# Hybrid decoder layer on one core: weight low parts and row products all on VectorE, output-projection weights in four quarters

## The chip, the cores and the metric

The kernel runs on 1 core of one Trainium2 chip. The metric is the device time of one execution in microseconds (us); lower is better. The engines of the core run in parallel, each working through its own queue in order: TensorE (PE, matmuls; PEld its weight loads), VectorE (DVE), ScalarE (ACT), GpSimd (POOL), and SyncE (SP), which issues the DMA transfers. They wait for one another through semaphores.

## The reference, cut to what matters

One decoder layer over 512 tokens of width 1024: a mixer with two attentions, a cross-attention into 256 memory rows, a mixture of experts, a final norm.

```python
h = _rms_norm(x, g_mix[l])
fq, fk, fv, f_logit, dq, dk, dv, gate_a, gate_b = jnp.split(h @ w_in[l], offsets, axis=-1)
...
y_a = _merge_heads(_fox_attention(...))      # 8 heads
y_b = _merge_heads(...)                      # 4 differential heads, rotary
merged = (jax.nn.sigmoid(gate_a) * (y_a @ w_branch_a[l])
          + jax.nn.sigmoid(gate_b) * (y_b @ w_branch_b[l]))
x = x + merged @ w_out[l]
x = x + _cross_attention(_rms_norm(x, g_cross[l]), _rms_norm(mem, g_mem[l]), w_cq[l], w_ckv[l], w_co[l])
hm = _rms_norm(x, g_ffn[l]).reshape(b * s, d)
x = x + _hier_moe(hm, ...).reshape(b, s, d)  # 32 experts, top 2
return _rms_norm(x, g_final)
```

## The kernel before

**Split products.** The big products ahead of the experts are done as three matmuls each (`mm3`, lines 278 to 280): both factors are cut in a high part and a low part. ACT makes the high part (`activation Copy`, L176), and a subtraction makes the low part (L177, `split`). For weights these are called `wh` and `wl`, for activations `hh`/`hl`, `mh`/`ml` and so on.

**The weight stream.** The class `Stream` (object `W`) cuts each weight into chunks of 1 MB and each chunk into two halves of 128x1024 elements. `load` has SP fetch a half into a raw buffer `wr`; `split` makes `wh` on ACT and `wl` either on VectorE or, for the halves whose number is in `self.pool`, on GpSimd. The set holds the numbers 12 to 63 without 57 and 59. `use(i, j)` makes sure that a chunk is split and asks, in `more`, for the next one. For the query weight of the cross-attention (`c_cq`) GpSimd also multiplies the raw half by a gain for each row (L143).

**Order.** It is written out by hand. At the start `nat_unit` runs four token tiles through the first weight chunk while `h_gain` (L326) multiplies the transposed input by `g_mix`, `h_split` makes its parts, and `h_stat` makes the row factors `rT`, which the small product `pR` spreads (L370). Then a loop of 24 iterations runs: 16 of `Fox` (4 head pairs by 4 query blocks of 128), 8 of `Diff`. Each does scores, softmax, multiplies of the probabilities by the reciprocal (L592 for Fox; L698 and L699 for Diff), a projection unit of weights (`unit()`, two in Diff), `W.more()`, the transposes `tf` or `td` (L275) and their copies (`pf` L603, `pd` L711), and the product with v one iteration later. Units of the first output branch (`br`, evacuated at L846) lie in the Diff iterations, so does `finish`, which transposes `zn` (`tz`, L745). After the loop come the remaining gate units and branch units; the last four branch units leave `mh` and `ml`, the merged activations, behind (L846, L853, L856, L857).

**The output projection.** `out_unit` adds `merged @ w_out` to x for token tile t and columns 256c to 256c+255: 8 contraction tiles by 3 matmuls of 256 columns into half a PSUM bank `wop` (tag "a", two buffers), then the addition (L1018). For c = 0 the tiles 0 and 1 go together. Tiles 2 and 3 are fillers: a list of steps as words (`U20` is `out_unit(2, 0)`) mixes them with the cross-attention (T, N, Q, K, S, M, P, A, O) and the routing. `W` in that list splits `c_co`. Then the experts run: 1 MB pages come through a ring of buffers, which PE frees, and PE multiplies them (`gu` L1410, `yd` L1432, `cb` L1450, `ga` L1238).

Of the kernel before, what the change touches and what calls it, by code (L numbers as in the profile page):

```python
# [10 lines left out]
F32 = mybir.dt.float32  # L11
# [4 lines left out]
OP = mybir.AluOpType  # L16
AX = mybir.AxisListType

P = 128
# [3 lines left out]
KD = D // P  # L23
# [15 lines left out]
def tile_hybrid_block(  # L39
# [5 lines left out]
    V, A, PE, G = nc.vector, nc.scalar, nc.tensor, nc.gpsimd  # L45
# [10 lines left out]
    def page(shape, dt, name):  # L56
        return pgp.tile(list(shape), dt, name=name, tag="pg")
# [3 lines left out]
    def work(shape, dt, name, tag="w"):  # L61
        return wk.tile(list(shape), dt, name=name, tag=tag, bufs=bufs[tag])
# [10 lines left out]
    def bank(name, tag):  # L73
        return ps.tile([P, 512], F32, name=name, tag=tag, bufs={"a": 2, "s": 4, "y": 2}[tag])
# [8 lines left out]
    def xt(t):  # L83
        return X[t // 2][:, t % 2]
# [6 lines left out]
    gm = c1.tile([P, KD], F32, name="gm")  # L91
# [14 lines left out]
    def xT(t, k0=0, n=KD):  # L106
        return XT[t // 2][:, t % 2, k0:k0 + n]
# [8 lines left out]
    class Stream:  # L116
        def __init__(self):
            self.spec, self.raw, self.hl = [], {}, {}
            self.loaded = self.done = self.next = 0
            self.lazy = False  # L120
            self.pool = set(range(12, 64)) - {57, 59}
            self.scale, self.new, self.land, self.ahead = {}, {}, {}, {}

        def add(self, src, k, n):
# [3 lines left out]
        def load(self, upto):  # L128

            while self.loaded < min(upto, 2 * len(self.spec), self.done + self.ahead.get(self.loaded // 2, NLD)):  # L130
                i, j = divmod(self.loaded, 2)
                src, k, n = self.spec[i]
                sl = slice(j * k // 2, (j + 1) * k // 2)
                if i in self.land:
                    if j == 0:
                        self.land[i] = page([P, k, n], F32, f"wr{i}")
                    raw = self.land[i][:, sl]
                else:
                    raw = work([P, k // 2, n], F32, f"wr{i}{j}", "ld")
                self.raw[self.loaded] = raw  # L140
                nc.sync.dma_start(raw, src[:, sl])
                if i in self.scale:
                    G.tensor_tensor(raw, raw, self.scale[i][:, sl, None].to_broadcast([P, k // 2, n]), op=OP.mult)  # L143
                self.loaded += 1

        def split(self, upto):

            while self.done < min(upto, 2 * len(self.spec)):
                i, j = divmod(self.done, 2)
                self.load(self.done + 1)  # L150
                _, k, n = self.spec[i]
                if j == 0:
                    self.hl[i] = [self.new.get((i, u), page)([P, k, n], F32R, f"w{u}{i}") for u in "hl"]
                hi, lo = self.hl[i]
                sl = slice(j * k // 2, (j + 1) * k // 2)
                n = k // 2 // 2 if self.done < 2 else k // 2
                for k0 in range(0, k // 2, n):
                    d = slice(sl.start + k0, sl.start + k0 + n)
                    split(hi[:, d], lo[:, d], self.raw[self.done][:, k0:k0 + n], G if self.done in self.pool else V)
                self.done += 1  # L160
                self.load(self.done + 4)

# [9 lines left out]

            self.split(self.next)

    def split(hi, lo, src, E=V):
        A.activation(hi, src, AF.Copy)  # L176
        E.tensor_tensor(lo, src, hi.bitcast(F32), op=OP.subtract)  # L177

    W = Stream()

# [96 lines left out]
    def mm3(o, lh, ll, rh, rl, first, last):  # L277
        PE.matmul(o, lh, rh, start=first, stop=False)  # L278
        PE.matmul(o, lh, rl, start=False, stop=False)  # L279
        PE.matmul(o, ll, rh, start=False, stop=last)  # L280
# [14 lines left out]
    def nat_unit(chunk, t, dst, d0, name, nt=1, tag="a"):  # L295

        wh, wl = W.use(chunk, t // 2)
        o = bank(f"{name}p{t}", tag)
        for i in range(nt):
            sl = slice((t + i) * P, (t + i + 1) * P)  # L300
            gemm(o[:, 256 * i:256 * i + 256], KD, lambda k: hk(HH, k, sl), lambda k: hk(HL, k, sl),
                 lambda k: wh[:, k, :], lambda k: wl[:, k, :])

        def evac():
            for i in range(nt):
                A.activation(dst[:, t + i, d0:d0 + 256], o[:, 256 * i:256 * i + 256], AF.Copy, scale=rT[:, t + i:t + i + 1])

        return evac
# [9 lines left out]
    def h_split(t, qs=(0, 1)):  # L318

        sl = slice(t * P, (t + 1) * P)  # L320
        for q in qs:
            split(HH[q][:, :, sl], HL[q][:, :, sl], xT(t, 4 * q, 4))

    def h_gain(t, E, k0=0, n=KD):
        v = xT(t, k0, n)
        E.tensor_tensor(v, v, gm[:, k0:k0 + n, None].to_broadcast([P, n, P]), op=OP.mult)  # L326

    def h_stat(t):
        rms_stat(xt(t), f"nx{t}", out=rT[:, t:t + 1])
# [5 lines left out]

    W.lazy = True
    lg = c1.tile([P, KD, 16], F32R, name="lg")
    h_gain(0, V, 0, 4)
    h_gain(0, G, 4, 4)
    h_split(0, (0,))  # L340
    W.split(1)
    h_split(0, (1,))
    W.split(2)
    evs = []
    for t in range(NT):
        evs.append(nat_unit(c_fv[0], t, fv, 0, "fv0", tag="as"[t // 2]))
        if t + 1 < NT:
            h_gain(t + 1, G)
            h_split(t + 1)
        if t == 1:  # L350
            split(lg[:, :, 0:8], lg[:, :, 8:16], lg_r)
            W.split(3)
        if t == 2:
            h_stat(0)
            h_stat(1)
            evs.pop(0)()
            evs.pop(0)()
            h_stat(2)
            h_stat(3)
# [474 lines left out]
    MH, ML = {}, {}  # L834
# [68 lines left out]
                for j in range(4):  # L903
                    units.append(lambda br_=br_, c=c, j=j: branch_unit(br_, c // 2, j))
    wov = w_out[0].rearrange("(k p) n -> p k n", p=P)
    c_wo = [W.add(wov[:, :, 256 * c:256 * c + 256], KD, 256) for c in range(4)]
    c_cq = W.add(w_cq[0].rearrange("(k p) n -> p k n", p=P), KD, 256)
    W.scale[c_cq] = gcc
    c_co = W.add(w_co[0].rearrange("(k p) n -> p k n", p=P), 2, D)
# [93 lines left out]

    W.new[c_co, "h"] = page2

    def out_unit(t, c, *more):

        wh, wl = W.hl[c_wo[c]]
        o = {}
        for u in (t, *more):  # L1010
            o[u] = bank(f"wop{c}{u}", "a")[:, 0:256]
            for k in range(KD - 1 if more else KD):
                out_part(o[u], u, wh, wl, k)
        for u in (t, *more):
            if more:
                out_part(o[u], u, wh, wl, KD - 1)
            xs = xt(u)[:, 256 * c:256 * c + 256]
            V.tensor_tensor(xs, o[u], xs, op=OP.add)  # L1018

    def out_part(o, t, wh, wl, k):  # L1020
        sl = slice(t % 2 * P, (t % 2 + 1) * P)
        mm3(o, MH[t // 2][:, k, sl], ML[t // 2][:, k, sl], wh[:, k, :], wl[:, k, :], k == 0, k == KD - 1)


    CX = {}
# [272 lines left out]

    EX = Experts()

    for c in range(4):
        W.use(c_wo[c], 1)
        if c == 0:
            out_unit(0, c, 1)
        else:
            out_unit(0, c)
            out_unit(1, c)
    W.split(2 * c_cq + 2)
    for step in """T0 N0 U20 Q0 U21 K0 T1 N1 U30 U22 W Q1 S0 M0 K1 U23 U31 N2 T2 S1 P0 Q2 M1 U32 A0 U33 K2 T3 O0 N3 S2
        M2 Q3 P1 X0 K3 F0 A1 S3 M3 P2 R0 O1 L0 P3 F1 z0.0 A2 X1 z0.1 A3 O2 z0.2 z0.3 R1 O3 L1 z0.4 z0.5 z1.0  # L1310
        E E E E H0 z0.6 H1 z1.1 z1.2 F3 X2 z0.7 z0.8 z1.3 z1.4 z0.9 z0.10 z1.5 z0.11 z1.6 z1.7 z0.12 z0.13 F2 z1.8
        R2 X3 L2 r0 z1.9 o0 H2 z2.0 z1.10 z1.11 z2.1 z1.12 z2.2 z2.3 z2.4 z1.13 R3 g0.0 z2.5 z2.6 r1 L3 z2.7
        z2.8 g0.1 z3.0 z2.9 o1 z2.10 z3.1 g0.3 z2.11 H3 z3.2 z2.12 z2.13 g0.2 g1.3 z3.3 r2 z3.4 g1.0 g1.1
        z3.5 z3.6 o2 z3.7 z3.8 z3.9 g1.2 z3.10 z3.11 g2.0 z3.12 z3.13 g2.1 g2.3 r3 g2.2 o3""".split():
        f, t = step[0], int(step[1]) if len(step) > 1 else 0
        if f == "U":
            out_unit(t, int(step[2]))
        elif f == "E":
            EX.load(page)
        elif f == "W":  # L1320
            W.split(2 * c_co + 2)
        elif f == "z":
            route_step(t)
        elif f == "g":
            gather0(t, int(step[3]))
        elif f == "M":
            cross_soft(t)
            cross_scale(t)
        else:
            {"N": lambda t: x_stat(t, "nc"), "F": ffn_stat, "r": ranks, "o": lambda t: onehot(0, t), "X": x_trans, "T": cross_trans, "Q": cross_q, "K": cross_qt, "S": cross_scores, "P": cross_ptrans,  # L1330
             "A": cross_av, "O": cross_out, "H": ffn_split, "R": router,
             "L": router_t}[f](t)
# [227 lines left out]
    for p in range(NE // 2):  # L1560
        q, qi = divmod(p, 2)
        more = q + 1 < NE // QUAD
        final = not more and qi == 1
        h = []
        for a in range(2):
            e = 2 * p + a
            sl = slice((2 * qi + a) * CAP, (2 * qi + a + 1) * CAP)
# [211 lines left out]
```

## Time and profile before

| | us |
|---|---|
| median of 3 runs | 1009.11 |
| lowest, highest | 1008.07, 1009.96 |
| the profiled execution, own time | 1009.81 |
| its span | 1008.1 |
| PE busy in the span | 966.5 (96%) |
| DVE busy | 457.2 (45%) |
| ACT busy | 308.6 (31%) |
| POOL busy | 200.3 (20%) |

The profiled execution takes 1.7 us more than its span. Busy shares are means over the span: the part ahead of the experts (to about 520 us) and the part with the experts have different loads. A timeline row gives the start, the length, the engine, the line, the operation, the tiles written and read, and in brackets how long the engine stood idle before it and what released it. A matmul's printed length has its way through the array in it; how fast a stream runs is read from one start to the next.

### The profile page before, as it was taken

How to read it: one execution, taken by the hardware profiler on the slowest of the kernel's cores; microseconds unless marked ns; L12 is line 12 of the kernel's file. 1: busy time of each engine (PE TensorE's matmuls, PEld its weight loads, DVE VectorE, ACT ScalarE, POOL GpSimd, SP SyncE). 2: the span in 40 equal slices, each digit the busy share in tenths (PEclk: the TensorE clock that was granted, in tenths of full speed). 3: DMA queues.
4: the chain of work that ended last, by engine and by line, in shares of the span. 5: the costliest groups of instructions: out<-in, count | busy, mean ns of one | idle time of the engine just before them, and what ended most of it. 6: DMA issues, size and time to landing. Idle time of an engine off the chain costs nothing. (4 is left out here: it accounts for less than half of the span.)

```text
span 1008.1 us, 13868 instructions
## 1 busy us (share of the span) xinstructions
PE 966.5 (96%) x5494; PEld 643.8 (64%) x5495; DVE 457.2 (45%) x967; ACT 308.6 (31%) x672; POOL 200.3 (20%) x245
## 2 busy tenths in 40 slices
PE   8999899999989999999799999999999999999985
PEld 7787677787878898998646536364453635436332
DVE  6554885846562526445632333323233332233335
ACT  5344444444353344245321112021121212112104
POOL 4841122223444555410100000000000000000003
PEclk8999999999999999999899999999999999999998
DMA  8221121121131247237389899999999999999902
GB/s 307 85 65 62 63 63 64 43 85 63 63 126 63 84 131 266 84 126 301 159 324 422 330 423 416 423 421 418 421 421 422 420 419 421 420 421 419 411 12 84
DMA packets 47862, 246.19 MB, mean 244 GB/s; under 512 B 4784, under 2 KB 12208, under 8 KB 23728
## 3 DMA queue, kind: packets, MB, share of 16 engines
q1 hardware_dynamic: 47648, 245.24, 61.4%
q8 instruction: 45, 0.74, 0.3%
q14 instruction: 25, 0.20, 0.1%
q10 hardware_dynamic: 144, 0.00, 0.0%
HBM read 243.13 MB, written 2.10 MB: 243 GB/s over the span
## 5 line engine op out<-in xcount | busy, mean ns | idle before, releaser
L1410 PE MATMUL gu<-gu,xg 128*64 128x512 f32 x960 | 210.5, 593 | 1.7 <-PEq L1479 1.6
L1410 PEld LDWEIGHTS gu<-gu,xg 128*64 128x64 f32 x960 | 72.9, 137 | 133.2 <-issue 121.1
L177 POOL TENSOR_TENSOR wl<-wr,wh 128x1024 fp32r<-128x1024 f32 x50 | 120.6, 2419 | 186.5 <-ACT wh L176 179.4
L1432 PE MATMUL yd<-dn,A 128*64 128x512 f32 x472 | 110.4, 596 | 0.0
L1454 DVE TENSOR_TENSOR xr<-cb,xr 128x512 f32<-128x512 f32 x120 | 75.7, 684 | 50.6 <-PE cb L1450 50.4
L1415 DVE SCALAR_TENSOR_TENSOR A<-A,gu 128x256 f32<-128x256 f32 x32 | 13.5, 421 | 176.1 <-ACT A L1414 176.1
L1550 POOL MEMSET A<- 128x128 f32 x1 | 0.2, 206 | 438.2 <-PE pth L275 438.2
L1432 PEld LDWEIGHTS yd<-dn,A 128*64 128x64 f32 x472 | 34.9, 137 | 64.3 <-issue 63.4
L1414 ACT ACTIVATE A<-gu 128x256 f32<-128x256 f32 x32 | 12.3, 385 | 201.2 <-PE gu L1410 201.2
L176 ACT ACTIVATE wh<-wr 128x1024 fp32r<-128x1024 f32 (+1 forms) x66 | 67.1, 1026 | 8.0 <-POOL wr L143 6.8
L1450 PE MATMUL cb<-Y,ohT 128*128 128x512 f32 x240 | 67.5, 412 | 0.9
L1440 DVE SCALAR_TENSOR_TENSOR Y<-yd,ws,Y 128x512 fp32r<-128x512 f32 x32 | 23.9, 750 | 91.8 <-ACT Y L1439 89.9
L1238 PE MATMUL ga<-G,hnh 128*128 128x256 f32 x256 | 64.6, 290 | 0.2 <-DVE ge L1358 0.2
L1238 PE MATMUL ga<-G,hnl 128*128 128x256 f32 x256 | 62.8, 283 | 0.0
L1439 ACT ACTIVATE Y<-yd,ws 128x512 fp32r<-128x512 f32 x32 | 21.9, 687 | 126.8 <-PE yd L1432 126.8
L1450 PEld LDWEIGHTS cb<-Y,ohT 128*128 128x128 f32 x240 | 42.7, 191 | 12.5 <-DVE xr L1454 3.2
L1238 PEld LDWEIGHTS ga<-G,hnh 128*128 128x128 f32 x256 | 48.5, 190 | 3.1 <-issue 2.4
L1238 PEld LDWEIGHTS ga<-G,hnl 128*128 128x128 f32 x256 | 48.6, 190 | 0.6
L1384 ACT ACTIVATE xg<-ga,smc 128x256 f32<-128x256 f32 x64 | 29.8, 475 | 52.3 <-PE ga L1238 52.3
L278 PE MATMUL wop<-wh,mh 128*128 128x256 f32 x128 | 36.9, 288 | 2.9 <-DVE xr L1018 1.8
L279 PE MATMUL wop<-wl,mh 128*128 128x256 f32 x128 | 36.4, 284 | 0.6 <-POOL wl L177 0.6
L280 PE MATMUL wop<-wh,ml 128*128 128x256 f32 x128 | 36.3, 283 | 0.0
(611 smaller groups left out, 1962.6 us busy)
## 6 DMA issues: line engine op xcount, KB each, us to landing
gu<-in_w_gu_dram SPq DMA_DIRECT2D x120, 1024.0 KB, 12.3
dn<-in_w_dn_dram SPq DMA_DIRECT2D x55, 1024.0 KB, 17.4
wr<-in_w_inp_dram SPq DMA_DIRECT2D x40, 512.0 KB, 3.7
Z<-in_w_gu_dram SPq DMA_DIRECT2D x8, 1024.0 KB, 14.8
wr<-in_w_out_dram SPq DMA_DIRECT2D x8, 512.0 KB, 6.5
Z<-in_w_dn_dram SPq DMA_DIRECT2D x4, 1024.0 KB, 19.8
dn<-in_w_dn_dram SPq DMA_DIRECT2D x6, 512.0 KB, 13.8
x<-in_x_dram SPq DMA_DIRECT2D x2, 1024.0 KB, 11.6
```

The source lines that it names most:

```text
L176: A.activation(hi, src, AF.Copy)
L177: E.tensor_tensor(lo, src, hi.bitcast(F32), op=OP.subtract)
L278: PE.matmul(o, lh, rh, start=first, stop=False)
L279: PE.matmul(o, lh, rl, start=False, stop=False)
L280: PE.matmul(o, ll, rh, start=False, stop=last)
L1238: PE.matmul(o, CX[u, t // 2][:, t % 2, kb * P:(kb + 1) * P], GQ[q][:, t].rearrange("p e s -> p (e s)"), start=(first and u == "h"), stop=( ...
L1384: A.activation(XG[q][:, kb], o, AF.Copy, scale=gfc[:, kb:kb + 1])
L1410: PE.matmul(gu[64 * f:64 * f + 64, :], xg(2 * i + j), w[:, :, j, 256 * f:256 * f + 256], start=(i + j == 0), stop=(i + j == 4))
L1432: PE.matmul(y[j][64 * a:64 * a + 64, :], hT[a][:, f % 2, f // 2], w(a, f)[:, j, f % 2], start=(f == 0), stop=(f == 3))
L1440: V.scalar_tensor_tensor(yl[rows, j], y[j][rows], ws, yh[rows, j].bitcast(F32), op0=OP.mult, op1=OP.subtract)
L1450: PE.matmul(banks[j], oh[:, t * P:(t + 1) * P], y[u][:, j], start=(u == 0), stop=(u == 1))
L1454: V.tensor_tensor(xs, banks[j], xs, op=OP.add)
```

## The change

Three things change. All halves of the weight stream get their low part on VectorE, the two row products of `c_cq` too, and `h_gain` as well: GpSimd makes none of them. The four chunks of `w_out` are no longer 8 contraction tiles by 256 columns but 4 contraction tiles by 512 columns (numbered 2c + kh for column half c and contraction half kh), so a matmul of the output projection has 512 columns, a bank is filled by two units, and one addition (now L1025) covers 512 columns. A new function `out_first` does tiles 0 and 1 for the first column half. In the list of steps `U20` and `U21` are the two contraction halves of the first column half of tile 2, `U22` and `U23` those of the second; the order of the U steps and the place of W are new. Lines in the new file are one lower than before up to about line 990 and 14 higher behind.

```diff
-            self.pool = set(range(12, 64)) - {57, 59}
...
-                    G.tensor_tensor(raw, raw, self.scale[i][:, sl, None].to_broadcast([P, k // 2, n]), op=OP.mult)
+                    V.tensor_tensor(raw, raw, self.scale[i][:, sl, None].to_broadcast([P, k // 2, n]), op=OP.mult)
...
-                    split(hi[:, d], lo[:, d], self.raw[self.done][:, k0:k0 + n], G if self.done in self.pool else V)
+                    split(hi[:, d], lo[:, d], self.raw[self.done][:, k0:k0 + n])
...
-    h_gain(0, V, 0, 4)
-    h_gain(0, G, 4, 4)
+    h_gain(0, 0, 4)
     h_split(0, (0,))
     W.split(1)
+    h_gain(0, 4, 4)
...
-            h_gain(t + 1, G)
+            h_gain(t + 1)
...
-    c_wo = [W.add(wov[:, :, 256 * c:256 * c + 256], KD, 256) for c in range(4)]
+    c_wo = [W.add(wov[:, 4 * kh:4 * kh + 4, 512 * c:512 * c + 512], 4, 512) for c in range(2) for kh in range(2)]
...
+    def out_unit(t, c, kh):
+
+        if kh == 0:
+            OB[t] = bank(f"wop{c}{t}", "a")
+        wh, wl = W.hl[c_wo[2 * c + kh]]
+        for k in range(4):
+            out_part(t, kh, k, wh, wl)
+        if kh == 1:
+            out_add(t, c)
...
+    def out_first():
+
+        for t in range(2):
+            OB[t] = bank(f"wop0{t}", "a")
+            for kh in range(2):
+                for k in range(4 - kh):
+                    out_part(t, kh, k, *W.hl[c_wo[kh]])
+        for t in range(2):
+            out_part(t, 1, 3, *W.hl[c_wo[1]])
+            out_add(t, 0)
...
+    for i in range(4):
+        W.use(c_wo[i], 1)
+        if i == 1:
+            out_first()
+        if i > 1:
+            out_unit(0, 1, i - 2)
+            out_unit(1, 1, i - 2)
     W.split(2 * c_cq + 2)
-    for step in """T0 N0 U20 Q0 U21 K0 T1 N1 U30 U22 W Q1 S0 M0 K1 U23 U31 N2 T2 S1 P0 Q2 M1 U32 A0 U33 K2 T3 O0 N3 S2
+    for step in """T0 N0 U20 Q0 U21 K0 T1 N1 U22 Q1 S0 M0 K1 U23 U30 W N2 T2 S1 U31 P0 Q2 M1 U32 A0 U33 K2 T3 O0 N3 S2
```

**VectorE in a Fox iteration** (the one whose multiplies start at 179.8 us before; `ri` is the reciprocal, `S` the probabilities, `dqk1l` and `r110a` evacuate a projection unit). Before:

```order
L589 RECIPROCAL ri_1926<-ls_1884 128x2
L592 TENSOR_SCALAR S_1875<-S_1875,ri_1926 128x384
L592 TENSOR_SCALAR S_1876<-S_1876,ri_1926 128x384
L177 TENSOR_TENSOR dqk1l<-dk1p_1895,dqk1h 128x512
L642 TENSOR_TENSOR r110a<-dk1p_1895,rot 128x512
L603 COPY pf_1948<-tf_1936 128x384
```

Now:

```order
L588 RECIPROCAL ri_1926<-ls_1884 128x2
L591 TENSOR_SCALAR S_1875<-S_1875,ri_1926 128x384
L591 TENSOR_SCALAR S_1876<-S_1876,ri_1926 128x384
L176 TENSOR_TENSOR wl_1931<-wr_1681,wh_1930 128x1024
L176 TENSOR_TENSOR dqk1l<-dk1p_1895,dqk1h 128x512
L641 TENSOR_TENSOR r110a<-dk1p_1895,rot 128x512
L602 COPY pf_1948<-tf_1936 128x384
```

The low part of a weight half stands behind the two multiplies and ahead of the evacuation and the copy.

**VectorE ahead of the output projection** (the last two branch units, `br_3811` and `br_3834`, and the first additions). Before:

```order
L846 SCALAR_TENSOR_TENSOR g_3469<-g_3469,br_3811 128x512
L853 TENSOR_TENSOR g_3469<-g_3469,g_2779 128x512
L857 SCALAR_TENSOR_TENSOR ml_3400<-g_3469,mh_3399 128x256
L857 SCALAR_TENSOR_TENSOR ml_3402<-g_3469,mh_3401 128x256
L846 SCALAR_TENSOR_TENSOR g_3469<-g_3469,br_3834 128x512
L853 TENSOR_TENSOR g_3469<-g_3469,g_2779 128x512
L857 SCALAR_TENSOR_TENSOR ml_3400<-g_3469,mh_3399 128x256
L857 SCALAR_TENSOR_TENSOR ml_3402<-g_3469,mh_3401 128x256
L1018 TENSOR_TENSOR xr_3758<-wop_3888,xr_3758 128x256
```

Now (`wl_3763` is w_out's chunk 0, `wl_3831` chunk 1):

```order
L176 TENSOR_TENSOR wl_3763<-wr_3700,wh_3762 128x1024
L845 SCALAR_TENSOR_TENSOR g_3469<-g_3469,br_3811 128x512
L852 TENSOR_TENSOR g_3469<-g_3469,g_2779 128x512
L856 SCALAR_TENSOR_TENSOR ml_3400<-g_3469,mh_3399 128x256
L856 SCALAR_TENSOR_TENSOR ml_3402<-g_3469,mh_3401 128x256
L176 TENSOR_TENSOR wl_3831<-wr_3730,wh_3830 128x1024
L845 SCALAR_TENSOR_TENSOR g_3469<-g_3469,br_3834 128x512
L852 TENSOR_TENSOR g_3469<-g_3469,g_2779 128x512
L856 SCALAR_TENSOR_TENSOR ml_3400<-g_3469,mh_3399 128x256
L856 SCALAR_TENSOR_TENSOR ml_3402<-g_3469,mh_3401 128x256
L176 TENSOR_TENSOR wl_3831<-wr_3766,wh_3830 128x1024
```

The low parts of chunk 0's second half and of both halves of chunk 1 now stand between the evacuations, one behind each unit.

**PE in `out_first`**, now (tile 0, contraction tiles 2 to 4; before, contraction tiles 0 to 6 of both tiles all read `wh_3762` and `wl_3763`):

```order
L277 MATMUL wop_3895<-wh_3762,mh_3399 128x512
L278 MATMUL wop_3895<-wl_3763,mh_3399 128x512
L279 MATMUL wop_3895<-wh_3762,ml_3400 128x512
L277 MATMUL wop_3895<-wh_3762,mh_3399 128x512
L278 MATMUL wop_3895<-wl_3763,mh_3399 128x512
L279 MATMUL wop_3895<-wh_3762,ml_3400 128x512
L277 MATMUL wop_3895<-wh_3830,mh_3399 128x512
L278 MATMUL wop_3895<-wl_3831,mh_3399 128x512
L279 MATMUL wop_3895<-wh_3830,ml_3400 128x512
```

From the 13th matmul on, tile 0 reads chunk 1; its second half (`wr_3766`) is read from the 19th on.

## Rows read from the trace of the kernel before

**Rows 1.** The page's busy times: engine, us, share, instructions.

```profile
PE 966.5 (96%) x5494; PEld 643.8 (64%) x5495; DVE 457.2 (45%) x967; ACT 308.6 (31%) x672; POOL 200.3 (20%) x245
```

**Rows 2.** PE's waits: who waited, for whom: us in total, times, longest.

```profile
PE tf L275 <- DVE S L592: 4.6, 6, 1.5
PE lg L1141 <- DVE hT L1135: 3.6, 1, 3.6
PE td L275 <- DVE T L699: 3.0, 4, 1.0
...
PE tz L745 <- DVE g L846: 0.5, 1, 0.5
```

**Rows 3.** Line 177, low parts: ns min/median/max, first and last start, shapes.

```profile
L177 POOL TENSOR_TENSOR wl<-wr,wh x50: 2380/2400/2640, 89.7 to 433.6; 128x1024 fp32r<-128x1024 f32 x50
...
L177 DVE TENSOR_TENSOR wl<-wr,wh x16: 684/1226/6802, 6.6 to 404.1; 128x1024 fp32r<-128x1024 f32 x12, 128x512 fp32r<-128x512 f32 x4
```

**Rows 4.** Timeline of DVE, 178 to 184 us (start, length, operation, idle before).

```profile
178.43 0.69 DVE L177 TENSOR_TENSOR dqk1l<-r101a,dqk1h 128x512 fp32r<-128x512 f32 x1 [0.76 <-ACT dqk1h L176]
...
179.83 2.87 DVE L592 TENSOR_SCALAR S<-S,ri 128x384 f32<-128x384 f32 x2
```

**Rows 5.** Timeline of POOL, the same stretch.

```profile
179.91 2.57 POOL L177 TENSOR_TENSOR wl<-wr,wh 128x1024 fp32r<-128x1024 f32 x1 [6.59 <-ACT wh L176]
```

**Rows 6.** Line 592 and line 853, all their instructions on DVE.

```profile
L592 DVE TENSOR_SCALAR S<-S,ri x32: 274/423/2605, 58.2 to 189.4; 128x128 f32<-128x128 f32 x8, 128x256 f32<-128x256 f32 x8, 128x384 f32<-128x384 f32 x8, 128x512 f32<-128x512 f32 x8
...
L853 DVE TENSOR_TENSOR g<-g,g x8: 692/1565/2865, 335.6 to 392.2; 128x512 f32<-128x512 f32 x8
```

**Rows 7.** Stretches: length, busy PE, PEld, DVE, ACT, POOL, granted clock, DMA, GB/s.

```profile
175.00:200.00 25.00, 23.60 (x153) 18.94 (x152) 21.32 (x46) 11.90 (x27) 5.75 (x3) 1.00 0.16 58
244.67:248.08 3.41, 1.83 (x15) 1.34 (x15) 3.38 (x6) 0.59 (x1) 0.14 (x1) 1.00 0.49 154
248.08:254.90 6.82, 6.82 (x25) 5.56 (x26) 4.60 (x17) 2.20 (x9) 0.00 (x0) 0.50 0.01 2
490.42:497.25 6.83, 5.92 (x26) 4.61 (x26) 3.65 (x19) 0.95 (x4) 2.38 (x10) 0.50 0.38 160
600.00:900.00 300.00, 299.34 (x1546) 145.62 (x1544) 96.91 (x180) 48.18 (x100) 0.00 (x0) 1.00 1.01 420
```

**Rows 8.** Timeline of DVE and of PE, 240 to 256 us.

```profile
242.42 2.93 DVE L699 SCALAR_TENSOR_TENSOR T<-T,dr,T 128x512 f32<-128x512 f32 x1
...
244.17 0.39 PE L280 MATMUL br<-yah,wl 128*128 128x512 f32 x1
245.50 0.63 PE L275 MATMUL td<-identf,T 128*128 128x128 f32 x4 [0.94 <-DVE T L699]
```

**Rows 9.** Timeline of PE, 386 to 392 us: last branch unit, first output products.

```profile
386.03 0.39 PE L280 MATMUL br<-ybh,wl 128*128 128x512 f32 x1
...
388.75 0.39 PE L280 MATMUL br<-ybh,wl 128*128 128x512 f32 x1
388.97 0.28 PE L278 MATMUL wop<-wh,mh 128*128 128x256 f32 x1
...
391.37 0.28 PE L280 MATMUL wop<-wh,ml 128*128 128x256 f32 x1
```

**Rows 10.** Timeline of ACT, 386 to 399 us.

```profile
395.67 1.05 ACT L176 ACTIVATE wh<-wr 128x1024 fp32r<-128x1024 f32 x1
```

**Rows 11.** Timeline of PE, 411 to 418 us: end of tiles 0 and 1.

```profile
417.19 1.04 PE L275 MATMUL tc<-identf,xr 128*128 128x128 f32 x8
```

**Rows 12.** Timeline of POOL, 6 to 18 us, and of ACT, 16 to 28 us.

```profile
9.71 6.84 POOL L326 TENSOR_TENSOR xT<-xT,gm 128x1024 f32<-128x1024 f32 x3 [1.51 <-DMA xT<-in_x_t_dram]
...
17.64 1.04 ACT L256 ACTIVATE nx_j<-x 128x1024 bf16<-128x1024 f32 x1
...
27.43 0.47 ACT L306 ACTIVATE fv<-fv0p,rT 128x256 f32<-128x256 f32 x1 [0.49 <-DVE rT L249]
```

**Rows 13.** SP's waits: who waited, for whom: us in total, times, longest.

```profile
SPq L1263 <- PE yd L1432: 181.2, 28, 16.3
```

More of the change, by code (lines that the diff above doesn't have):

```diff
@@ L173, in more, with split @@
             self.split(self.next)
-    def split(hi, lo, src, E=V):
+    def split(hi, lo, src):
         A.activation(hi, src, AF.Copy)
-        E.tensor_tensor(lo, src, hi.bitcast(F32), op=OP.subtract)
+        V.tensor_tensor(lo, src, hi.bitcast(F32), op=OP.subtract)
     W = Stream()
@@ L322, in h_split, with h_gain @@
             split(HH[q][:, :, sl], HL[q][:, :, sl], xT(t, 4 * q, 4))
-    def h_gain(t, E, k0=0, n=KD):
+    def h_gain(t, k0=0, n=KD):
         v = xT(t, k0, n)
-        E.tensor_tensor(v, v, gm[:, k0:k0 + n, None].to_broadcast([P, n, P]), op=OP.mult)
+        V.tensor_tensor(v, v, gm[:, k0:k0 + n, None].to_broadcast([P, n, P]), op=OP.mult)
     def h_stat(t):
@@ L1004, in tile_hybrid_block, with out_part, out_add @@
     W.new[c_co, "h"] = page2
[L1006 to L1020, printed above, removed]
-        sl = slice(t % 2 * P, (t % 2 + 1) * P)
-        mm3(o, MH[t // 2][:, k, sl], ML[t // 2][:, k, sl], wh[:, k, :], wl[:, k, :], k == 0, k == KD - 1)
+    OB = {}
+    def out_unit(t, c, kh):
[6 more added lines that the diff above has]
+            out_add(t, c)
+    def out_part(t, kh, k, wh, wl):
+        sl = slice(t % 2 * P, (t % 2 + 1) * P)
+        mm3(OB[t], MH[t // 2][:, 4 * kh + k, sl], ML[t // 2][:, 4 * kh + k, sl], wh[:, k, :], wl[:, k, :],
+            kh + k == 0, kh + k == 4)
+    def out_add(t, c):
+        xs = xt(t)[:, 512 * c:512 * c + 512]
+        V.tensor_tensor(xs, OB[t], xs, op=OP.add)
+    def out_first():
[7 more added lines that the diff above has]
+            out_add(t, 0)
     CX = {}
@@ L1299, in tile_hybrid_block @@
     EX = Experts()
[L1301 to L1307, printed above, removed]
+    for i in range(4):
[5 more added lines that the diff above has]
+            out_unit(1, 1, i - 2)
     W.split(2 * c_cq + 2)
-    for step in """T0 N0 U20 Q0 U21 K0 T1 N1 U30 U22 W Q1 S0 M0 K1 U23 U31 N2 T2 S1 P0 Q2 M1 U32 A0 U33 K2 T3 O0 N3 S2
+    for step in """T0 N0 U20 Q0 U21 K0 T1 N1 U22 Q1 S0 M0 K1 U23 U30 W N2 T2 S1 U31 P0 Q2 M1 U32 A0 U33 K2 T3 O0 N3 S2
         M2 Q3 P1 X0 K3 F0 A1 S3 M3 P2 R0 O1 L0 P3 F1 z0.0 A2 X1 z0.1 A3 O2 z0.2 z0.3 R1 O3 L1 z0.4 z0.5 z1.0
@@ L1316, in tile_hybrid_block @@
         if f == "U":
-            out_unit(t, int(step[2]))
+            out_unit(t, *divmod(int(step[2]), 2))
         elif f == "E":
```

## The prediction, on record before the changed kernel ran

> **What bounds the kernel now.** I read the page's busy times first: PE works 96% of the span, DVE 45% [rows 1]. So time is lost only where PE waits, where its clock is halved, or in matmuls that could be fewer; an engine that has room is worth asking only when it makes PE wait. Second, PE's waits by releaser [rows 2]: apart from the routing (`lg`, 3.6 us) the large ones are the transposes `tf` behind the multiplies of line 592 (4.6 us in 6 waits) and `td` behind line 699 (3.0 us in 4). Third, why DVE is late there, the timelines of DVE and POOL side by side [rows 4, 5]: two multiplies of the same shape take 2.87 us together while POOL's low part runs from 179.91 for 2.57 us. Line by line the same thing shows as a spread: line 592 from 0.27 to 2.61 us, line 853 from 0.69 to 2.87 [rows 6], one low part on DVE 6.80 us where the median is 1.23 [rows 3]. DVE's long instructions end where POOL's do. What has to be weighed is 50 low parts of 2.40 us on POOL against 50 of about 1.23 us in DVE's own queue [rows 3], the stretch at half clock behind some waits, and the matmul count. Fourth, the stretches [rows 7]: from 600 to 900 us PE is busy 299.3 of 300 us with the DMA engines full beside it.
>
> **The change part by part.** Everything is reckoned against the profiled execution, 1009.8 us, which is 0.7 us above the median.
>
> *Cover on DVE.* From 175 to 200 us DVE is busy 21.3 of 25 us and POOL makes three low parts [rows 7]. Each of those lengthened one multiply by about 2.1 us (2.87 less twice 0.38, [rows 4, 6]). Without them DVE is at 21.3 - 6.3 = 15.0, with three low parts of 1.23 at 18.7. So DVE gets less work there than before, not more, though in another order.
>
> *Fox iterations.* The low part now stands behind the multiplies, so `tf` no longer waits for it; the evacuation and the copy behind it start about 0.7 us earlier than before (1.23 instead of 2.1). Of the 4.6 us the longest wait, 1.5, has no low part of POOL beside it and stays. A printed wait of 0.94 costs 1.10, since the starts of 244.17 and 245.50 lie 1.33 apart where 0.23 is usual [rows 8]; so five waits of 3.1 us together are worth 3.9. I leave 0.4 for waits that a late copy may make: **-3.5**. Bounds: -3.9, and 0 if the copies take it back.
>
> *Diff iterations.* The `td` waits (3.0, with four restarts 3.6) go, as line 699 falls from 2.93 [rows 8] to about 0.75 (2.93 less the same 2.1). But here the low part, 1.23, stands ahead of line 846 and of the copy `pd`, which release `tz`, `br` and the next scores. `tz` already waits 0.5 [rows 2] in the second of the two places; I put 0.6 more on it and 0.2 on `br`, and 1.0 on the scores in the first: **-1.8**. Bounds: -3.6 and 0.
>
> *Matmul count.* Twelve branch matmuls of 512 columns take 388.75 - 386.03 = 2.72, 0.227 each; twenty of 256 columns take 391.37 - 388.97 = 2.40, 0.120 each [rows 9]. The output projection has 384 of the short ones, now 192 long ones: 46.1 against 43.5 us, half of it in tiles 0 and 1, half in the fillers. The fillers give **-1.3**; U30 takes a bank that a `cq` held and has no new wait by the order of the instructions.
>
> The page "TensorE: Matmul & The Clock Gate" of the Trainium skill, section "Back-to-back issue gap", states a gap of N/2.4 ns and about 2.5 ns more. By it the saving would be 41.9 - 41.4 = 0.5 us in all; at both lengths the rows of this trace lie about 11 ns above that figure, so a long matmul saves more here, and the rows decide.
>
> *Tiles 0 and 1.* Before, from 388.97 to the transposes at 417.19 [rows 9, 11]: 28.2 us, of which 192 x 0.120 = 23.0 are matmuls and 5.2 lost. Now matmuls take 96 x 0.227 = 21.8. What is lost is new: `out_first` wants chunk 1 for its 13th matmul and the second half of chunk 1 for its 19th. That half's high part ended at 396.7 [rows 10]. The two line-853 sums ahead of it shrink by 2.2 each [rows 6]; two low parts of 1.23 come in between, each waiting some 0.6 for its high part: 396.7 - 4.4 + 3.7 = 396.0, its low part 397.3. PE gets to chunk 1 at 391.7, waits 0.9 for the low part of its first half (392.9), 1.9 for the high part of the second, 0.9 for the low part, 0.3 for the first addition; with restarts 4.6. 21.8 + 4.6 = 26.4: **-1.8**. Bounds: -5.2 - 1.3 = -6.5 if chunk 1 is ready, +1 if it is 3 us later. The row products of `c_cq` wait for a transfer on DVE behind the additions, and nothing of PE's is due behind them.
>
> *Start.* The gains leave POOL, where three took 6.84 us to 16.55 [rows 12]. On DVE each is about 1.23, the size of a low part [rows 3], but in one queue with the low parts; the last one ends at about 20.7, since it stands behind the low part of the second chunk, which waits for ACT. The four sums of squares, 17.64 before, start at about 21.9, and the last row factor, 27.3 before [rows 12], comes at about 30.5 (of the 9.7 us between them 1.1 were waits for DVE). PE reaches `pR`, which reads it, at about 29: **+1.2** after 0.3 from faster low parts at the first tile. Bounds: -1, and +4 for the full delay.
>
> *Nowhere else.* Branch and gate units from 317 to 389 us have no wait of PE; low parts there take 1.23 in a queue that is half empty. In the expert part SP waits for PE to free pages (181 us for `yd` alone, [rows 13]) and PE's waits [rows 2] have no row for a page, so what PE gains in front moves the end.
>
> Sum: 1.2 - 3.5 - 1.8 - 1.8 - 1.3 = -7.2; 1009.8 - 7.2 = 1002.6, and about 1002 on the median.
>
> **The rivals.** *A new half-clock stretch.* Before, a wait of 3.6 us (`lg`) was followed by 6.83 us at 0.50, that is 1.2 GHz; the two `td` waits near 245, in 3.41 us with PE busy 1.83, by another [rows 2, 7]. Such a stretch costs half of itself, 3.4 us. In `out_first` PE stands still 3.7 of about 5.6 us. For it: that is more idle time than near 245. Against: the matmuls between these waits are long ones, where those near 245 are small. Time: 1002 + 3.4 = 1005.4. *The stretch at 248 goes.* Its waits shrink from two to one of about 1.0 among small matmuls; 1002 - 3.4 = 998.6. That both happen gives my forecast again.
>
> *Slower: DVE's order becomes the bound.* In the Fox and Diff loop, some 27 low parts stand ahead of the copy and of the next softmax. DVE idled 0.76 before the last evacuation [rows 4]; if nothing but that takes them up, each holds PE by 1.23 - 0.76 = 0.47, 12.7 us in all, and the 3.5 and 1.8 don't come: 1009.1 + 1.2 + 12.7 - 3.1 = 1020. It decides once DVE's work between two multiplies is longer than PE's, that is over 25 us in that window; 18.7 speaks against it. A part of it ends at 1011.
>
> *No change.* If the multiplies were long for another reason than POOL's low parts, or pages came to bind the experts, the gains vanish and 2 us of matmuls against 1.2 at the start remain: about 1008.5. Against it: the two ends of rows 4 and 5, 0.2 us apart, and SP's waits.
>
> **How the numbers follow.** Forecast 1002 (own range 999.5 to 1004): 0.46, with no change in the number of half-clock stretches. New stretch, 1005.4: 0.22. The one at 248 gone, 998.6: 0.18. No change, 1008.5: 0.06. DVE as bound, 1011 to 1020: 0.08. The range goes from 998.6 less 3 (start bound -1, out-projection bound) to 1005.4 plus 2.6 (start bound +4): 995.5 to 1008. About 0.2% is what a measurement of this kernel can tell from no change, 2 us. Faster: 0.46 + 0.18 + 0.19 of the new-stretch case = 0.83; same 0.03 + 0.05 = 0.08; slower 0.08 and 0.01 of the no-change case = 0.09.
>
> **What would show it.** Right: line 592 within 0.27 to 0.5 us everywhere, no row of `tf` behind it but one of about 1.5; `td` behind line 699 gone; `tz` and the scores behind line 846 and `pd` with about 1 us each; `wop` waiting about 0.9, 1.9 and 0.9 us for chunk 1; `pR` waiting about 1.5 us; from 600 us on the trace as before, only earlier. Wrong: long multiplies without a low part on POOL; evacuations late in every iteration; a page for which PE waits; a half-clock stretch at another place, which moves the time by 3.4 us each.

## The result, and the profile after

The changed kernel takes 1002.25 us (median of 8 runs, 999.86 to 1005.17); the kernel before takes 1008.46 beside it (8 runs, 1005.18 to 1010.37). The ratio is 0.994 with a 95% interval of 0.9919 to 0.996: faster, by about 6 us, with 1002 forecast. The profiled execution of after is one of the slower of its eight: 1004.69 us, span 1002.9. The steps below are read from it, against 1009.81 and 1008.1 of before.

The page's busy times of after answer to [rows 1]: POOL lost 126 us, DVE gained only 16, and PE works 3.8 us less.

```profile
PE 962.7 (96%) x5302; PEld 632.0 (63%) x5303; DVE 473.2 (47%) x1015; ACT 308.7 (31%) x672; POOL 73.9 (7%) x189
```

DVE took 50 low parts, two row products and four gains (one of them half as wide) for 16 us because its other instructions became shorter. The lines of after that answer to [rows 3] and [rows 6] (ns min/median/max): no multiply above 0.55 us, no sum above 0.69, no low part above 1.49.

```profile
L176 DVE TENSOR_TENSOR wl<-wr,wh x66: 682/1225/1487, 6.4 to 436.8; 128x1024 fp32r<-128x1024 f32 x62, 128x512 fp32r<-128x512 f32 x4
...
L591 DVE TENSOR_SCALAR S<-S,ri x32: 274/413/550, 57.9 to 186.2; 128x128 f32<-128x128 f32 x8, 128x256 f32<-128x256 f32 x8, 128x384 f32<-128x384 f32 x8, 128x512 f32<-128x512 f32 x8
...
L852 DVE TENSOR_TENSOR g<-g,g x8: 691/692/694, 332.2 to 389.4; 128x512 f32<-128x512 f32 x8
```

The place of [rows 4] in after, in DVE's timeline: the two multiplies take 0.75 us where they took 2.87, and the low part comes behind them.

```profile
177.70 0.75 DVE L591 TENSOR_SCALAR S<-S,ri 128x384 f32<-128x384 f32 x2
...
178.37 1.22 DVE L176 TENSOR_TENSOR wl<-wr,wh 128x1024 fp32r<-128x1024 f32 x1
```

PE's waits of after (us in total, times, longest) answer to [rows 2]. `tf` has its long wait and one of 0.4 left, `td` has no row any more; new are `sd` behind `pd`, a longer `tz`, and `wop` behind chunk 1.

```profile
PE lg L1155 <- DVE hT L1149: 3.6, 1, 3.6
...
PE tf L274 <- DVE S L591: 1.9, 2, 1.5
...
PE sd L542 <- DVE pd L710: 1.9, 3, 1.2
PE wop L277 <- ACT wh L175: 1.6, 1, 1.6
...
PE tz L744 <- DVE g L845: 1.6, 1, 1.6
...
PE wop L278 <- DVE wl L176: 0.8, 2, 0.5
...
PE pR L369 <- DVE rT L248: 0.6, 1, 0.6
PE br L277 <- DVE g L845: 0.5, 1, 0.5
...
PE w12p L277 <- DVE g L845: 0.4, 1, 0.4
```

The stretches of after answer to [rows 7] (length, busy PE, PEld, DVE, ACT, POOL, granted clock, DMA share, GB/s). Ahead of the experts before had one of 6.83 us at 0.50, that is 1.2 GHz, at 248 and one at 490 (and one in the start, at 12.56). After has four, of 3.41 and of 6.83; those at 296.23 and 391.80 are new, and the one at 391.80 follows 6.52 us in which PE was busy 4.56. The last row shows that the expert part stands as before, with the DMA engines full.

```profile
245.03:248.44 3.41, 3.41 (x10) 2.63 (x9) 2.13 (x10) 2.19 (x9) 0.00 (x0) 0.50 0.10 35
296.23:299.64 3.41, 3.41 (x9) 2.63 (x8) 1.43 (x2) 0.00 (x0) 0.00 (x0) 0.50 0.57 205
385.28:391.80 6.52, 4.56 (x20) 3.12 (x19) 4.52 (x9) 3.39 (x7) 0.00 (x0) 1.00 0.70 244
391.80:398.63 6.83, 6.37 (x14) 4.70 (x15) 3.57 (x3) 5.14 (x5) 0.00 (x0) 0.50 0.53 154
487.38:490.79 3.41, 3.41 (x18) 2.69 (x16) 1.60 (x10) 0.00 (x0) 1.31 (x6) 0.50 0.38 159
...
600.00:900.00 300.00, 299.33 (x1546) 145.62 (x1544) 96.90 (x180) 48.18 (x100) 0.00 (x0) 1.00 1.01 420
```

Where the time went, by PE's first instruction of each stage. In the column "clock", half the busy PE time of each half-clock stretch of the stage is taken for what the stretch costs; the last column is the change without it. That is an estimate from the granted clock of 0.50. The trace of e1 (below), which has the Diff code of after, bears it out in Diff: 3.41 us less at half clock, and 114.58 us instead of 116.44.

| stage | before, us | after, us | change | clock before, after | change without clock |
|---|---|---|---|---|---|
| start, to `fq0p` | 29.84 | 29.64 | -0.2 | not counted | -0.2 |
| Fox, to the first `sd` | 162.82 | 158.83 | -4.0 | 0, 0 | -4.0 |
| Diff, to `w10p` | 116.43 | 116.44 | 0.0 | 3.4, 3.4 | 0.0 |
| gates and branches, to `wop` | 79.88 | 80.37 | +0.5 | 0, 0 | +0.5 |
| tiles 0 and 1, to `tc` | 28.22 | 28.44 | +0.2 | 0, 3.2 | -3.0 |
| fillers, to `co` | 40.25 | 39.32 | -0.9 | 0, 0 | -0.9 |
| routing, to `gu` | 52.83 | 51.92 | -0.9 | 3.0, 1.7 | +0.4 |
| experts, to the end | 497.80 | 497.96 | +0.2 | not counted | +0.2 |
| sum | 1008.07 | 1002.92 | -5.1 | | -7.0 |

### The profile page after: what moved, and what is told of

It is laid out like the page before. It is cut to its first block, busy times and chain, and to the rows that moved or that the text cites. A ratio compares the mean times of both kernels' runs of the same rounds, so it can differ in the third digit from the quotient of the medians.

```text
span 1002.9 us, 13451 instructions
## 1 busy us (share of the span) xinstructions
PE 962.7 (96%) x5302; PEld 632.0 (63%) x5303; DVE 473.2 (47%) x1015; ACT 308.7 (31%) x672; POOL 73.9 (7%) x189
## 5 line engine op out<-in xcount | busy, mean ns | idle before, releaser
L176 DVE TENSOR_TENSOR wl<-wr,wh 128x1024 fp32r<-128x1024 f32 (+1 forms) x66 | 78.5, 1195 | 34.2 <-ACT wh L175 33.6
L277 PE MATMUL wop<-wh,mh 128*128 128x512 f32 x64 | 26.9, 420 | 1.8 <-ACT wh L175 1.6
L278 PE MATMUL wop<-wl,mh 128*128 128x512 f32 x64 | 26.4, 412 | 0.8 <-DVE wl L176 0.8
L583 ACT ACTIVATE S<-S,bi 128x128 f32<-128x128 f32 (+3 forms) x32 | 17.8, 555 | 30.0 <-DVE bi L580 30.0
```

What stands on the lines that cost most here:

```text
L176: V.tensor_tensor(lo, src, hi.bitcast(F32), op=OP.subtract)
```

## Experiments

Theory A says that GpSimd's reads and writes stretch DVE's instructions, so that nearly all of the gain comes from the low parts. The rivals: the gain comes from the 512-column output weights; or from another order on DVE, for which POOL's work is of no matter.

**e1: only the low parts move.** The kernel before, with

```diff
-            self.pool = set(range(12, 64)) - {57, 59}
+            self.pool = set()
```

> The kernel before with one edit: all weight low parts on VectorE. Gains, row products and the 256-column output weights stay as before. Theory A (what counted was that GpSimd's low parts lengthened VectorE's multiplies): no multiply of line 592 over 0.6 us, tf waits down from 4.6 to about 1.9 us, the first Diff scores about 4 us earlier than before, the output projection of tiles 0 and 1 shorter than its 28.2 us because line 853 falls to 0.69 and nothing waits for chunk 1: about 25 us; together about 1008.5 - 4 - 3 = 1001.5. Rival B (the output weights carry a good half of the gain): about 1005 to 1006.

Measured: 1001.16 us (6 runs), ratio 0.9932 (0.9907 to 0.9958), as much as the whole change. Multiplies and waits up to the output projection are those of after: `tf` 1.9, no `td`, `tz` 1.6. In the projection PE waits for a `g` (1.4) and for no weight.

```profile
PE tf L275 <- DVE S L592: 1.9, 2, 1.5
PE tz L745 <- DVE g L846: 1.6, 1, 1.6
...
PE wop L278 <- DVE g L846: 1.4, 1, 1.4
```

Tiles 0 and 1, with their short matmuls and old order, take 25.5 us at full clock where before took 28.2, so a part of what that stage can win is the low parts' as well (its stretch from the first `wop` to `tc`):

```profile
383.14:408.63 25.49, 23.54 (x193) 23.13 (x193) 15.61 (x22) 10.67 (x13) 4.65 (x2) 1.00 0.38 123
```

**e2: only the output projection changes.** After, with the low parts, the row products and the gains back on GpSimd:

```diff
+            self.pool = set(range(12, 64)) - {57, 59}
...
+                    split(hi[:, d], lo[:, d], self.raw[self.done][:, k0:k0 + n], G if self.done in self.pool else V)
```

> The changed kernel with the low parts of the same 50 halves, the row products and the gains back on GpSimd: only the output weights and the order of the fillers are changed. Theory A: Fox and Diff as before; the matmuls of the output projection save 2.6 us, but out_first waits for chunk 1, whose low parts GpSimd makes 1.2 us slower and behind longer line-852 sums, about 6 us of waits against 5.2 lost before; a new half-clock stretch there costs 1.7 to 3.4 more. About 1008 to 1010, no gain. Rival B: 1005 to 1006.

Measured: 1010.22 us (12 runs), ratio 1.0004 (0.9985 to 1.0024): no gain. The waits of [rows 2] are all back, and `out_first` waits for two low parts of GpSimd, with a half-clock stretch of 10.24 us behind the first, so tiles 0 and 1 take 31.3 us.

```profile
PE tf L275 <- DVE S L592: 4.5, 6, 1.5
PE wop L279 <- POOL wl L177: 3.6, 2, 1.9
PE td L275 <- DVE T L699: 3.0, 4, 1.0
```

That stretch of e2:

```profile
394.89:405.13 10.24, 8.36 (x20) 5.70 (x19) 1.99 (x3) 6.77 (x8) 8.40 (x10) 0.50 0.32 103
```

The low parts bring the gain, and the long matmuls, as the change orders them, give back what they save.

**e3: GpSimd reads beside DVE's low parts.** After, with 50 subtractions on GpSimd that nobody waits for, each of one high part from itself (`h`):

```diff
+                    G.tensor_tensor(gh, h, h, op=OP.subtract)
```

> The changed kernel with one idle instruction more for each of the 50 halves: GpSimd subtracts the high part from itself into a buffer that nobody reads. The orders of PE, VectorE and ScalarE stay. Theory A (GpSimd's reads of SBUF hold VectorE's multiplies up): line 591 goes back to 2.5 us at the longest, tf and td waits come back and, with the low part in VectorE's queue too, are longer than before: about 1002.3 + 6 to 9 = 1008 to 1011. Rival C (the order in VectorE's queue made the difference, not the contention): 1002.3, waits as in the changed kernel.

Measured: 1027.42 us (4 runs), ratio 1.0188 (1.0158 to 1.0218). The direction is theory A's; the size, 25 us on after, is about three to four times what I expected. Long multiplies are back beside a subtraction of GpSimd: here, in the timelines of DVE and of POOL, 2.38 us beside 2.02.

```profile
183.70 2.38 DVE L596 TENSOR_SCALAR S<-S,ri 128x384 f32<-128x384 f32 x2
```

```profile
183.85 2.02 POOL L161 TENSOR_TENSOR gh<-wh 128x1024 f32<-128x1024 f32 x1 [7.79 <-ACT wh L178]
```

The low parts, 50 of which before makes on GpSimd, now lengthen on DVE too, up to 2.92 us:

```profile
L179 DVE TENSOR_TENSOR wl<-wr,wh x66: 684/1225/2920, 6.6 to 458.0; 128x1024 fp32r<-128x1024 f32 x62, 128x512 fp32r<-128x512 f32 x4
```

and PE's waits of e3 are longer than those of before ([rows 2]) for `wop`, as long for `tf` and `td`:

```profile
PE tf L279 <- DVE S L596: 4.8, 6, 1.5
PE wop L282 <- ACT wh L178: 2.9, 2, 2.6
PE td L279 <- DVE T L703: 2.8, 2, 1.4
```

The trace has no wait for one of these subtractions, and the orders of PE, DVE and ACT are those of after: the contention alone makes the difference. The "SBUF — State Buffer" page of the Trainium skill, section "Who interferes with whom", says that DVE and GpSimd share a pair of ports, and that where both need it the later instruction is blocked until the earlier has ended. The rows above agree: the second of the two multiplies ends at 186.08, GpSimd's subtraction 0.21 earlier, at 185.87. Other instructions of DVE that start inside a GpSimd instruction do the same in before and e3, the longer ones by more: multiplies end 0.08 to 0.28 us behind it, line-853 sums (857 in e3) 0.55, low parts 1.08 of their own 1.23. By stage e3 loses 7.5 us in Fox, 7.1 in Diff, 3.7 in gates and branches and at most 1.3 in each other stage ahead of the experts. Of the 25 us some 7 are half-clock time (30.7 us of such stretches ahead of the experts against 17.1 in after, each taken to cost half of itself); the split of the rest into single waits I did not settle.

**e4: another order in `out_first`.** After, but both tiles do contraction tiles 0 to 5 first, then 6 and 7 of both, so that chunk 1's second half is wanted by the 37th matmul instead of the 19th:

```diff
-            for kh in range(2):
-                for k in range(4 - kh):
-                    out_part(t, kh, k, *W.hl[c_wo[kh]])
+            for k in range(6):
+                out_part(t, k // 4, k % 4, *W.hl[c_wo[k // 4]])
...
-            out_part(t, 1, 3, *W.hl[c_wo[1]])
+            for k in (2, 3):
+                out_part(t, 1, k, *W.hl[c_wo[1]])
```

> The changed kernel with another order in out_first: contraction tiles 0 to 5 of both token tiles first, then 6 and 7 of both, so that the second half of chunk 1 is wanted 24 matmuls (5.4 us) after chunk 0 is through. Theory A: the waits for chunk 1 (0.4, 1.6, 0.5 us) shrink to about 0.5, and with them the half-clock stretch from 391.8 goes: the output projection of tiles 0 and 1 falls from 28.4 to about 23, the time to about 1002.3 - 5.5 = 997. Rival D (the stretch comes from elsewhere or the next wait takes their place): about 1000 to 1002.

Measured: 997.22 us (6 runs), ratio 0.9888 (0.9863 to 0.9913), as expected. The stage takes 23.0 us at full clock where after takes 28.4; PE has two short waits in it (its stretch, then the rows of PE's timeline).

```profile
384.71:407.71 23.00, 22.38 (x97) 17.82 (x97) 16.91 (x20) 10.67 (x13) 0.00 (x0) 1.00 0.47 152
```

```profile
388.21 0.50 PE L278 MATMUL wop<-wl,mh 128*128 128x512 f32 x1 [0.37 <-DVE wl L176]
...
396.71 0.47 PE L277 MATMUL wop<-wh,mh 128*128 128x512 f32 x1 [0.25 <-DVE xr L1025]
```

In after, PE's timeline has these rows at the same place; the second starts the half-clock stretch:

```profile
388.77 0.50 PE L278 MATMUL wop<-wl,mh 128*128 128x512 f32 x1 [0.36 <-DVE wl L176]
...
391.80 0.80 PE L277 MATMUL wop<-wh,mh 128*128 128x512 f32 x1 [1.60 <-ACT wh L175]
...
393.06 0.80 PE L278 MATMUL wop<-wl,mh 128*128 128x512 f32 x1 [0.47 <-DVE wl L176]
```

So the order made both the waits and, in the profiled executions, the half clock: 5.4 us in the stage and 5.0 between the medians.

**e5: in Diff, high and low part move behind the copies.** e4, and in the Diff iterations

```diff
-        W.more()
-        if isinstance(it, Diff):
+        if isinstance(it, Fox):
+            W.more()
+        else:
...
             ev = unit()
-            W.more()
         it.trans()
...
             it.copy()
             ev()
+            W.more()
```

A Diff iteration called `W.more()` twice, ahead of the first unit's evacuation and behind the second unit; now one call behind the second unit's evacuation makes what both made.

> The kernel of the new out_first order (997.2 us) with one edit more: in the Diff iterations the weight halves are split behind the copy and the evacuation of the second unit, not ahead of them. Theory E (the Diff stage gained nothing in the changed kernel because the low part, 1.23 us, stands ahead of line 845 and of the copy pd, for which tz, br and the scores then wait 1.7, 0.7, 1.4 and 0.8 us): these four shrink to 0.5, 0.2, 0.3 and 0, the stretch at half clock near 296 goes in part: 997.2 - 3.5 = 993.7, and the low parts in their new place delay only the next softmax, which has room. Rival F (the waits only move to the multiplies of the next iteration, td behind line 698): 997.

Measured: 1005.46 us (8 runs), ratio 0.9962 (0.9946 to 0.9979): 8 us slower than e4, so this theory of mine (E) fell. `tz` does fall to 0.5 and the `sd` waits go, but ACT's high part now comes late as well, often two of them one behind the other, and PE waits for it and for the low part in the units, and for `td` again.

```profile
PE td L274 <- DVE T L698: 1.9, 4, 0.6
PE br L277 <- ACT wh L175: 1.2, 2, 0.6
PE br L279 <- DVE wl L176: 1.1, 2, 0.5
PE w01p L277 <- ACT wh L175: 0.9, 1, 0.9
PE w00p L277 <- ACT wh L175: 0.7, 1, 0.7
...
PE tz L744 <- DVE g L845: 0.5, 1, 0.5
```

The Diff stage takes 120.0 us without any half-clock stretch; in after it is 113.0 once its two stretches are taken out.

**e6: the gains back on GpSimd**, on e4 (`h_gain` with its engine argument as before).

> The kernel of the new out_first order with one edit more: the gains of the input tiles back on GpSimd, as in the kernel before. Theory G (the gains on VectorE made the row factors late, so that pR waits 1.2 to 1.4 us): pR no longer waits, the low parts of the first tiles are lengthened again as they were before, and the first fq0p starts at about 29.4 instead of 30.3: 997.2 - 0.9 = 996.3, which only the profile can tell. Rival H (the lengthened low parts cost as much): no change in fq0p.

Measured: 996.80 us (6 runs), ratio 0.9877 (0.9853 to 0.99). `pR` no longer waits and `fq0p` starts at 29.60 instead of e4's 30.27; the intervals of e4 and e6 overlap, so in the time 0.7 us can't be told apart. Nor does the start show it for sure: e8, below, has the same start as e6, no wait of `pR` either, and `fq0p` at 30.27. **e7**, e5 and e6 together:

> Both edits of e5 and e6 on the kernel of the new out_first order. If the two stages are independent of each other and of the rest: 997.2 - 3.5 - 0.9 = 992.8. If gains in front are lost further on, in the routing or to the expert pages: 995 to 996.

Measured: 1004.76 us (8 runs), ratio 0.9943 (0.9922 to 0.9963), e5's loss again, and `fq0p` 1.1 us earlier than in e5.

**e8: in Diff only the low part moves.** e6; ACT's high part stays where it was, the subtraction alone, and with it the request for the next load, goes behind the copy and the evacuation:

```diff
+        if isinstance(it, Diff):
+            W.held = []
         W.more()
...
             it.copy()
             ev()
+            W.low()
```

> The kernel with the new out_first order and the gains on GpSimd (996.8 us) with one edit more: in the Diff iterations ScalarE makes the high part at its old place, and only VectorE's low part is moved behind the copy and the evacuation of the second unit. Theory E, mended after the run that moved both parts (there PE waited for the high part): tz 0.5, br 0.2, scores 0.3 and 0 instead of 1.7, 0.7, 1.4 and 0.8, and the first product with a low part behind them waits 0 to 0.5: w10p starts 2 to 3.5 us earlier after the first Diff scores than there (it was 114.6 us), the time is about 994. Rival F (the low parts are wanted as soon as they are made): waits of br, w00p or w01p for line 176 take it back, 997 or more.

Measured: 994.75 us (5 runs), ratio 0.9873 (0.985 to 0.9895), the fastest of all. DVE's timeline has the copy and the evacuation ahead of the low part:

```profile
243.10 0.68 DVE L723 COPY pd<-td 128x512 f32<-128x512 f32 x1
243.70 0.68 DVE L858 SCALAR_TENSOR_TENSOR g<-g,br 128x512 f32<-128x512 f32 x1
244.29 1.22 DVE L183 TENSOR_TENSOR wl<-wr,wh 128x1024 fp32r<-128x1024 f32 x1
```

and PE's waits in Diff are `td` again, but short, with `br` and `tz` at 0.5:

```profile
PE td L287 <- DVE T L711: 1.7, 4, 0.6
...
PE br L290 <- DVE g L858: 0.5, 1, 0.5
PE tz L757 <- DVE g L858: 0.5, 1, 0.5
```

Diff takes 111.2 us in the trace against 114.6 in e6, of which 1.7 is a half-clock stretch that e6 has at 243.71 and e8 has not. Its time can't be told from e6's (the intervals overlap, and the profiled executions have spans of 994.1 and 994.2: e8's start, routing and experts are 0.7, 0.8 and 1.9 longer); that it beats both kernels of the case can.

## Why the prediction was right

The total came out: 1002.25 against 1002, and the direction for the reason named. Its terms did so less well than the sum; they add up to -7.2, and without the clock the table has -7.0. That the two agree so closely is luck: Diff came out 1.8 us worse than its term, the start 1.4 and tiles 0 and 1 1.2 better, and what the trace shows with the clock is -5.1.

- **Mechanism: right.** No multiply of line 592 above 0.55 us (0.5 forecast), line 853 at 0.69 everywhere. e1 and e3 show the cause from both sides.
- **Fox, -3.5: right,** -4.0 measured. The rest of `tf` is 1.9, as forecast a wait of 1.5 and little beside it. The cover on DVE held: PE's longest wait for a copy `pf` is 0.3 us. The rival that DVE's order becomes the bound did not come.
- **Diff, -1.8: wrong, 0.0 without the clock.** `td` went as forecast, but the low part ahead of `g` and `pd` costs more: `tz` 1.6 instead of 1.1 and `sd` 1.9 instead of 1.0. The 0.2 more on `br` did not come: it waits 0.5 for `g` in before, at the same place, and 0.5 in after. So 3.0 us of `td` waits went, and 1.1 of `tz` and 1.9 of `sd` came. The term took 0.6 of the 1.23 for `tz`; the timelines below this list show a whole low part ahead of the evacuation that it waits for. e8 puts the low part behind and gets 111.2, which is 1.8 below 113.0, but with other waits than the term had: 1.7 of `td` are left and those of `sd` behind DVE are gone.
- **Matmul count, fillers -1.3: near,** -0.9. No wait of PE in that stage is over 0.2 us.
- **Tiles 0 and 1, -1.8: the term was mis-sized, and a rival came on top.** Of the 3.7 us of waits forecast for chunk 1 (4.6 with the first addition and the restarts), 2.4 are printed (0.36, 1.60, 0.47): the waits for the low parts came at about half of their forecast. Without the clock the stage is 3.0 shorter by the estimate above, so better than forecast. But the first rival, a half-clock stretch in `out_first` (chance 0.22), happened in this execution: 3.2 us, and the gain was gone. The rival's 1005.4 is near this execution's 1004.69, though a shorter stretch in the routing (-1.3) and the start, which did not cost, are in that number too. Whether the executions nearer to 1000 lack the stretch is not shown, as they have no trace. With the wide weights e4's order takes 23.0 us, with the narrow ones e1 takes 25.5: the order decides whether the width pays.
- **Start, +1.2: not borne out,** -0.2 in this trace. The last gain ends at 19.85 instead of 20.7, and `pR` waits 0.6 instead of 1.5. The wait does come from the gains: it stands in all four traces with the gains on DVE (0.6 to 1.2 us in after, e3, e4 and e5) and in none of the others. What it costs is not shown: `fq0p` starts at 29.64 to 30.27 in those four, and at 28.90 to 30.27 where only the low parts have moved to DVE and the gains are GpSimd's (e1, e6, e7, e8). The half-clock stretch at 12.56 of before is missing in after, which may hide a part.
- **Nowhere else: nearly right.** The experts are unchanged (+0.2). Not foreseen was +0.5 in gates and branches, the same 0.5 in e1, where only low parts moved; the row that shows it is `w12p` with 0.4 among the waits above. A part of the +0.4 in the routing may be the estimate's: the stage takes 52.8 us in the three traces with one stretch of 6.83 us (before, e3, e8) and 51.6 to 51.9 in the five with one of 3.41, where the estimate has 1.3 between before and after.
- **The stretch at 248:** it became half as long, where the second rival had it go, and a new one of 3.41 us stands at 296.23, behind the `tz` and `br` waits. The forecast "no change in the number of half-clock stretches" did not hold: ahead of the experts three became four, and their sum fell from 20.5 us to 17.1.

The wait of `br` in before, which [rows 2] does not show:

```profile
PE br L278 <- DVE g L846: 0.5, 1, 0.5
```

DVE's timeline of after at the second place in Diff:

```profile
292.25 0.69 DVE L735 TENSOR_TENSOR zn<-zo,rq_z 128x512 f32<-128x512 f32 x1
292.85 1.22 DVE L176 TENSOR_TENSOR wl<-wr,wh 128x1024 fp32r<-128x1024 f32 x1
293.99 0.68 DVE L845 SCALAR_TENSOR_TENSOR g<-g,br 128x512 f32<-128x512 f32 x1
```

PE's timeline of the same place:

```profile
294.72 0.66 PE L744 MATMUL tz<-identf,zn 128*128 128x128 f32 x4 [1.59 <-DVE g L845]
295.92 0.55 PE L277 MATMUL br<-yah,wh 128*128 128x512 f32 x1 [0.54 <-DVE g L845]
```

Half-clock stretches differ from kernel to kernel even where the code is the same. The runs of one kernel spread by about 5 us, the size of one to three such stretches; where they lay is known for the one profiled execution of each alone. The mean granted clock of every execution is on record and goes with the time, but not alone: in after it is 0.986 at 1004.69, 1004.81 and 1005.17 us and 0.992 at 1000.09, in e4 0.988 at 999.45 and 0.994 at 994.88, yet after's 999.86 has 0.987.

## What to carry to other kernels

Before work is given to an idle GpSimd, read the maximum beside the median of VectorE's lines: a 2 us stretch of one multiply on the path costs more than the subtraction in VectorE's own queue. Where such work is put back on VectorE, its place in the queue decides: behind what TensorE waits for next, and apart from the step on ScalarE that has to stay early (e8 against e7). After a change of weight shape, look which matmul is the first to need each half: six contraction tiles of both outputs first instead of seven of one was worth 5 us; the shape in the order of the change was worth nothing (after against e1).

## What was not expected of the hardware

- Half-clock stretches came in lengths of 3.41, 6.83 and 10.24 us, and behind stretches in which PE was only partly idle: 1.83 us busy of 3.41 [rows 7], 4.56 of 6.52 in after. In e2 PE was busy only 8.36 of the 10.24 us at half clock, with a wait for GpSimd in it.
- One low part on DVE took 6.80 us before [rows 3], where GpSimd was busy with instructions one behind the other from 401.34 to 409.80; in after, none takes over 1.49.
- Fifty GpSimd subtractions that nobody waits for cost 25 us, about four times what taking the low parts away from it had gained. It is not that more was stretched: 30 of DVE's instructions in e3 are over 0.5 us longer than the median of the same ones in after, by 40 us together, and 25 in before, by 49 us. In e3 eleven of them are low parts, which stand in DVE's own queue; that this is the reason was not tested.
- Not all of DVE was stretched. The evacuation of `br` (line 850 in e3), which reads PSUM, took 0.68 or 0.69 us in all 16 cases, five of them wholly inside a GpSimd subtraction.
